# Neighbourhood attention in a two-layer diffusion backbone: keys of six heads loaded once and copied on the chip, and patterns without their unused columns

## Chip, cores, metric

The kernel runs on one core of a Trainium2 chip. The metric is the device time of one execution in microseconds. An execution is also profiled: the profile's span runs from the first to the last instruction.

## The reference

Two layers over 2048 tokens of width 1024 on a 32 x 64 grid, with 256 context tokens. The first layer joins a convolution branch and grouped-query attention; the second joins a Fourier branch and a neighbourhood attention, and the change lies in the latter alone. It has 8 heads of 64 channels. Each query at grid position (r, w) looks at 8 rows x 16 columns of keys around it, with a learned bias by relative position, and at all 256 context tokens:

```python
s_win = jnp.einsum('brqhd,brkwhd->bhrqkw', qg, kb).astype(jnp.float32) * scale \
    + bias.astype(jnp.float32)[None]
s_win = jnp.where(col_ok[:, None, :], s_win, NEG_INF).reshape(Bq, H, rows, GRID_W, kr * GRID_W)
s_ctx = jnp.einsum('brqhd,bchd->bhrqc', qg, kc).astype(jnp.float32) * scale
p = jax.nn.softmax(jnp.concatenate([s_win, s_ctx], axis=-1), axis=-1).astype(v.dtype)
...
o = jnp.einsum('bhrqkw,brkwhd->brqhd', p_win, vb) + jnp.einsum('bhrqc,bchd->brqhd', p_ctx, vc)
```

## The kernel before

The stage of interest is `natten` (L1502). Its work is cut into 32 units (h, t): head h from 0 to 7 (the title and the change count heads from 1, the code from 0), and t one of four bands of 16 grid columns. A unit has four blocks of 128 queries (8 rows x 16 columns), and a block sees 256 context keys and a window of 12 or 16 rows x 32 columns, 640 or 768 keys in all.

**Operands.** Numbers are held as a sum of two reduced-precision parts, hi and lo. The query tile `nq` [128, 2048] holds 64 channels of hi in partitions 0 to 63 and 64 channels of lo in partitions 64 to 127. Two key tiles, `nk0` (hi) and `nk1` (lo), each [128, 2304], hold the same 64 channels twice, once in each half, so that one matmul sums (hi + lo) of the query with one part of the key. All come from DRAM, where earlier stages put them (`q2_d`, `k2_d`). Each parity of h has one buffer of `nq`, `nk0` and `nk1` (pools `nk0` and `nk1`): a head's tiles take the place of those of two heads earlier, once the last score of that head has read them.

**Patterns.** The negated bias, with a huge number where a key is out of reach, lies ready in DRAM (`pat_d`). Three tiles `pat` [128, 3, 768] hold it, one per kind of band (bands 1 and 2 share one): 256 zeros for the context, then 512 window columns for each of three kinds of block. Blocks of the first and the last kind have 640 columns in all and read columns 0 to 639.

**Loads.** `load_keys(u)` (L1535) is called when the scores of the unit before u begin. For t = 0 it loads the head's queries (two DMAs of 512 KB) and keys (four of 576 KB: two parts, each into both halves); for t other than 2 it loads a pattern (768 KB). All issues of `load` have line L1539. `load_values(u)` loads the 8 x 128 values `nv` of a unit in four DMAs of 128 KB (L1571), with three buffers, and once per head those of the context (`nvc`, L1566). All stand in SP's queue. The order in SP's queue is made by a planner from program order and simulated times; only loads of the first five units keep program order.

**The stream** (L1756). TensorE, ScalarE, VectorE and GpSimd keep the order written out by hand. A unit is six steps. In step j of unit i, TensorE transposes probabilities of unit i (L1657), ScalarE and VectorE split them into hi and lo (L1662, L1664), and TensorE multiplies values with products transposed five steps earlier (L1677, L1678); scores (L1599, L1603) are made some two and a half units ahead of these, and the first score of head h comes in step 24h - 15, counted over all units from 0 as `now = 6 * i + j` (step 3 of unit 4h - 3); the last one, of its unit t = 3, in step 24h + 8. A score is evicted with its pattern by VectorE (L1611), its exponential taken by ScalarE three steps later (L1618), and scaled by GpSimd two steps after that (L1626). At a unit's end ScalarE copies the result (L1691), a DMA brings its other half to the right partitions (`ny`, L1692), and GpSimd adds the halves ten steps later (L1695). `extra(i, j)` is called at the end of each step and loads the next stage's weights near the end.

Of the kernel before, what the change touches and what calls it, by code (L numbers as in the profile page):

```python
# [11 lines left out]
F32 = mybir.dt.float32  # L12
F32R = mybir.dt.float32r
# [7 lines left out]
P = 128  # L21
D = 1024
KT = D // P
S = 2048
L = 256
T = S + L
# [3 lines left out]
HEADS = 8  # L30
# [53 lines left out]
class Build:  # L84
# [1417 lines left out]
    def natten(self):  # L1502
        nc = self.nc
        with ExitStack() as es:
# [3 lines left out]
            kp = [None, self.pool(self.n_es, "nk1", 1, side="right")]  # L1508
# [14 lines left out]
            units = [(h, t) for h in range(HEADS) for t in range(4)]  # L1523
# [3 lines left out]
            pats = []  # L1527
            for i in range(3):
                p = bp.tile([P, 3, 768], F32, name=f"pat{i}")
                nc.gpsimd.memset(p[:, :, 0:256], 0.0)  # L1530
                pats.append(p)
            heads, vals, ctxs, probs, youts, left = {}, {}, {}, {}, {}, {}

            def load_keys(u):
                h, t = u  # L1535
                first = u in units[:5]

                def load(dst, src):
                    ins = nc.sync.dma_start(dst, src)  # L1539
                    if first:  # L1540
                        self.tc.keep_in_program_order(ins)

                m, r0 = h // 2, (h % 2) * 64
                if t == 0:
                    qt = kp[h % 2].tile([P, S], F32R, name="nq", tag="nq")
                    load(qt[0:64].bitcast(F32), self.q2_d[m][0, r0 : r0 + 64])
                    load(qt[64:128].bitcast(F32), self.q2_d[m][1, r0 : r0 + 64])
                    ks = []
                    for a in range(2):
                        k = kp[h % 2].tile([P, T], F32R, name=f"nk{a}", tag=f"nk{a}")  # L1550
                        for r in range(2):
                            load(k[r * 64 : r * 64 + 64].bitcast(F32), self.k2_d[m][a, r0 : r0 + 64])
                        ks.append(k)
                    heads[h] = (qt, ks)
                if t != 2:
                    kind = kind_of[t]
                    load(
                        pats[kind][:, :, 256:768],
                        self.pat_d[:, h].rearrange("(r k) p c -> k p r c", k=3)[kind],
                    )  # L1560

            def load_values(u):
                h, t = u
# [14 lines left out]
            def scores(u):  # L1578

                h, t = u  # L1580
                if u == units[0]:
                    load_keys(u)
                if following(u):
                    load_keys(following(u))
                probs[u] = []
                for i in range(4):
                    pr = prp.tile([P, 768], F32, name="npr", tag="npr")
                    probs[u].append(pr)
                    left[id(pr)] = 1
                    yield (lambda i=i, pr=pr: score(h, t, i, pr))  # L1590
# [117 lines left out]
            def first_block():  # L1708

                bias.close()  # L1710
                qp = self.pool(self.n_es, "nq0", 1, side="right")
                y = qp.tile([P, KT, 256], F32, name="y0")
                yh, yl = (qp.tile([P, KT, 256], F32R, name=f"y0{a}") for a in "hl")
                gz = yl[:].bitcast(F32)
                self.first = y, yh, yl
                nc.sync.dma_start(gz, self.gz2_d[:, :, 0:256].rearrange("c p t -> p c t"))
                for g in range(4):
                    nc.sync.dma_start(y[:, g], self.yc_d[g][:, 0:256])
                    if g < 3:
                        nc.sync.dma_start(y[:, 4 + g], self.yd_d[g][:, 0:256])  # L1720
                for _ in range(Q1):
                    yield
                for k in range(7):
                    nc.gpsimd.tensor_tensor(out=y[:, k], in0=y[:, k], in1=gz[:, k], op=ALU.mult)
                    if k % 2 == 1 or k == 6:
                        yield
                        ks = slice(k & 6, k + 1)
                        nc.scalar.activation(yh[:, ks], y[:, ks], AF.Copy)
                        yield
                        nc.vector.tensor_tensor(  # L1730
                            out=yl[:, ks], in0=y[:, ks], in1=yh[:, ks].bitcast(F32), op=ALU.subtract
                        )

            def extra(i, j):
                if (i, j) == (28, 5):
                    even.close()
                    wo = self.pool(self.n_es, "nwo", 1, side="right")
                    self.wout = [wo.tile([P, KT, 512], F32R, name=f"wout2{a}") for a in range(2)]
                now = 6 * i + j
                k, r = divmod(now - WO0, WO1)  # L1740
                if r == 0 and 0 <= k < KT:
                    f = self.load_wout_part(self.wout_raw(wor), self.I["cd_w_out"][0], k, 0, nc.vector)
                    next(f)
                    parts.append((now + WO2, f))
                for f in [f for d, f in parts if d == now]:
                    next(f, None)
                if now == Q0:
                    parts.extend((Q0 + d, f) for f in [first_block()] for d in range(20))
                    next(parts[-1][1])

            self.stream(q, units, scores, [4] * len(units), steps, transposes, multiply, LAG, OFF, True, extra)
            for _, f in parts:
                next(f, None)
# [142 lines left out]
```

## Time and profile before

| | us |
|---|---|
| three runs | 2920.73, 2907.32, 2914.79 (median 2914.79) |
| the profiled execution | 2907.36 |
| its span | 2905.6 |
| neighbourhood attention, first score to last unit's result | 2388.7 to 2718.6 of the span |
| engines, busy share of the span | TensorE 95%, VectorE 63%, GpSimd 49%, ScalarE 38% |
| granted TensorE clock, mean | 0.977 of full speed |

A busy TensorE is not TensorE at its peak, since its matmuls are pipelined and overlap in the records. The DMA share is the mean busy share of the core's 16 DMA engines; it can pass 1, as transfers on one engine overlap. In the views PE is TensorE, PEld its weight loads, DVE VectorE, ACT ScalarE, POOL GpSimd and SP the engine whose queue issues most transfers.

### The profile page before, as it was taken

Reading aid. Unit: us, or ns where it says so; the run is one execution under the profiler, and the core shown is the slowest. Engines: PE = TensorE matmul, PEld = TensorE weight load, DVE = VectorE, ACT = ScalarE, POOL = GpSimd, SP = SyncE. Lnnn points to the kernel's source line nnn. Section 1 sums busy time; section 2 is a strip of 40 time slices with the busy share of each in tenths; the row PEclk is TensorE's granted clock in tenths of the full one; section 3 lists DMA queues with packets and bytes.
Section 4 is the critical chain, followed back from the end, with each engine's and each line's share of the span. In section 5 each row is a group of like instructions: output and inputs, shape, how many; then the busy total and the mean of one; then the engine's idle time right before and its main releaser. Section 6 shows DMA issues by size and latency. Waiting matters only on the chain.

```text
span 2905.6 us, 40946 instructions
## 1 busy us (share of the span) xinstructions
PE 2752.1 (95%) x14481; PEld 2118.0 (73%) x14481; DVE 1825.2 (63%) x2867; ACT 1116.8 (38%) x2081; POOL 1416.4 (49%) x1151
## 2 busy tenths in 40 slices
PE   7998799999999999999999999999999997889898
PEld 5988799996444444444447788988898876788787
DVE  4798868898777878878977454101212246777563
ACT  3223120312445555555553223123222236677321
POOL 2568610711666787887885652222222214445342
PEclk9999899998999999999999999999999998999999
DMA  9546332474533433321216543333434269998862
GB/s 297 192 131 207 129 123 97 135 239 151 149 107 103 144 98 106 120 68 44 73 33 210 192 159 143 138 112 112 143 132 136 82 197 230 235 230 196 270 210 80
DMA packets 346808, 432.27 MB, mean 149 GB/s; under 512 B 55900, under 2 KB 260236, under 8 KB 341611
## 3 DMA queue, kind: packets, MB, share of 16 engines
q1 hardware_dynamic: 310891, 403.03, 46.2%
q10 hardware_dynamic: 35712, 26.62, 2.9%
q8 instruction: 114, 1.87, 0.3%
q14 instruction: 91, 0.75, 0.1%
HBM read 281.87 MB, written 152.84 MB: 150 GB/s over the span
## 4 chain that ended last, share of the span: by engine, by line
PE 62%; DMA 10%; DVE 3%; POOL 2%; issue 2%; ACT 1%; SPq 0%; POOLq 0%; ACTq 0%; DVEq 0%
PE av L922 9%; PE s L907 8%; PE mm L431 6%; PE mm L433 6%; PE mm L432 6%; PE m L884 6%; PE mo L1107 4%; PE mo L1108 4%; PE mo L1109 4%; DMA nv<-v_d 3%; DMA nk<-k 3%; PE mm L442 1%; PE mm L441 1%; PE mm L440 1%; DMA pat<-pat_d 1%
## 5 line engine op out<-in xcount | busy, mean ns | idle before, releaser
L886 DVE TENSOR_REDUCE ast<-m 128x1 f32<-128x512 f32 (+1 forms) x656 | 397.9, 626 | 145.9 <-PE m L884 143.8
L912 ACT ACTIVATE pr<-s 128x512 f32<-128x512 f32 x584 | 343.2, 595 | 311.7 <-PE s L907 269.6
L947 POOL TENSOR_TENSOR accp<-accp,pr 128x512 f32<-128x512 f32 x283 | 400.1, 1414 | 86.0 <-ACT pr L912 71.3
L447 POOL TENSOR_TENSOR wlo<-wraw,whi 128x1024 fp32r<-128x1024 f32 x64 | 202.4, 3169 | 380.3 <-ACT whi L446 380.2
L533 DVE SCALAR_TENSOR_TENSOR acc<-u,cw,acc 128x1151 f32<-128x1151 f32 (+1 forms) x240 | 353.0, 1526 | 0.0
L922 PE MATMUL av<-pr,vt 128*64 128x512 f32 x1168 | 315.7, 619 | 0.0
L433 PE MATMUL mm<-hi_ab,wlo 128*128 128x384 f32 x768 | 258.7, 338 | 16.8 <-POOL wlo L447 15.5
L432 PE MATMUL mm<-lo_ab,whi 128*128 128x384 f32 x768 | 259.8, 339 | 0.0
L431 PE MATMUL mm<-hi_ab,whi 128*128 128x384 f32 x768 | 256.2, 340 | 3.3 <-ACT hi_ab L380 1.9
L431 PE MATMUL mm<-hi_cd,whi 128*128 128x512 f32 x640 | 250.8, 392 | 1.1 <-ACT hi_cd L380 1.1
L432 PE MATMUL mm<-lo_cd,whi 128*128 128x512 f32 x640 | 250.1, 391 | 0.4 <-DVE lo_cd L381 0.4
L433 PE MATMUL mm<-hi_cd,wlo 128*128 128x512 f32 x640 | 246.7, 390 | 0.0
L947 DVE TENSOR_TENSOR accd<-accd,pr 128x512 f32<-128x512 f32 x165 | 169.2, 1026 | 1.3 <-DVE accd L947 0.5
L1664 DVE TENSOR_TENSOR nlo<-npt,nhi 128x512 fp32r<-128x512 f32 x192 | 123.6, 645 | 69.3 <-ACT nhi L1662 68.5
L884 PEld LDWEIGHTS m<-k1h,q 128*128 128x128 f32 x328 | 61.8, 188 | 133.8 <-DVE ast L886 79.8
L433 PEld LDWEIGHTS mm<-hi_ab,wlo 128*128 128x128 f32 x768 | 145.5, 190 | 17.8 <-POOL wlo L447 15.8
L884 PEld LDWEIGHTS m<-k0h,q 128*128 128x128 f32 x328 | 63.5, 196 | 125.2 <-DVE ast L886 82.1
L1626 POOL TENSOR_SCALAR npr<-npr,nst 128x640 f32<-128x640 f32 (+1 forms) x128 | 108.0, 857 | 89.5 <-DVE nst L1625 64.1
L372 DVE TENSOR_SCALAR ht<-ptr,scale,shift 128x384 f32<-128x384 f32 (+2 forms) x96 | 61.2, 671 | 141.1 <-PE ptr L369 140.5
L431 PEld LDWEIGHTS mm<-hi_ab,whi 128*128 128x128 f32 x768 | 144.9, 190 | 5.3 <-ACT hi_ab L380 2.9
L432 PEld LDWEIGHTS mm<-lo_ab,whi 128*128 128x128 f32 x768 | 145.4, 189 | 0.9 <-issue 0.8
L431 PEld LDWEIGHTS mm<-hi_cd,whi 128*128 128x128 f32 x640 | 120.4, 188 | 26.1 <-ACT hi_cd L380 1.6
(321 smaller groups left out, 6931.4 us busy)
## 6 DMA issues: line engine op xcount, KB each, us to landing
wraw<-in_cd_w_in_dram SPq DMA_DIRECT2D x46, 512.0 KB, 3.8
pat_d<-big SPq DMA_DIRECT2D x72, 256.0 KB, 4.0
nk<-k SPq DMA_DIRECT2D x32, 576.0 KB, 12.7
pat<-pat_d SPq DMA_DIRECT2D x24, 768.0 KB, 6.0
nv<-v_d SPq DMA_DIRECT2D x128, 128.0 KB, 7.3
adaraw<-in_ab_w_ada_dram SPq DMA_DIRECT2D x24, 512.0 KB, 8.2
adaraw<-in_cd_w_ada_dram SPq DMA_DIRECT2D x24, 512.0 KB, 3.7
w_d<-whi SPq DMA_DIRECT2D x22, 512.0 KB, 2.8
```

The lines of the kernel that those rows point to most:

```text
L431: nc.tensor.matmul(ps, a, hh[:, k, cols], start=k == 0, stop=False)
L432: nc.tensor.matmul(ps, a, hl[:, k, cols], start=False, stop=False)
L433: nc.tensor.matmul(ps, b, hh[:, k, cols], start=False, stop=k == KT - 1)
L447: (eng or nc.vector).tensor_tensor(out=lo, in0=src, in1=hi.bitcast(F32), op=ALU.subtract)
L533: ins = nc.vector.scalar_tensor_tensor(out=acc[:, :n], in0=u[:, tap : tap + n], scalar=cw[:, ch, tap : tap + 1], in1=acc[:, :n], op0=ALU.m ...
L884: nc.tensor.matmul(ps[:, :n], lhs, kt[hp // 2][0][:, a : a + n], start=True, stop=True)
L886: nc.vector.tensor_reduce(out=s["st"][:, qt, col : col + 1], in_=ps[:, :n], axis=AX.X, op=ALU.min)
L907: nc.tensor.matmul(ps[:], kt[hp // 2][key][:, k * P : k * P + P], s[x][:].rearrange("p j n -> p (j n)"), start=key == 0, stop=key == 1,)
L912: nc.scalar.activation(pr[:], ps[:], AF.Exp, scale=-1.0)
L922: nc.tensor.matmul(s["av"][x * 64 : x * 64 + 64], vt[:, k - 1 + x, kv * 64 : kv * 64 + 64], s["pr"][k - 1 + x][:], start=k == 1, stop=k == ...
L947: eng.tensor_tensor(out=s[name][:], in0=first_in[:], in1=s["pr"][k][:], op=ALU.add)
L1664: return lambda: nc.vector.tensor_tensor(out=lo[:, :o], in0=pt[:, :o], in1=hi[:, :o].bitcast(F32), op=ALU.subtract)
```

## The change

Queries and keys get their own function, `load_head`. For heads 0 and 1 it loads as before, both halves of each key tile; head 1's loads now come when unit (0, 2) is prepared, ahead of the pattern of unit (0, 3). For heads 2 to 7 it loads the lower half of each key tile only, and it is called one head earlier in the program, when unit (h, 0) is prepared for head h + 1. The upper half is written by GpSimd: twelve copies of 64 x 384 (six for each of the two key tiles), one at the end of each of the twelve steps from 24h - 4 to 24h + 7, for head h + 1. Each pattern load becomes two DMAs: the first and the last kind of block without their last 128 columns, which no eviction reads, and the middle kind whole.

```diff
+            def load_head(h, whole):
+                m, r0 = h // 2, (h % 2) * 64
+                qt = kp[h % 2].tile([P, S], F32R, name="nq", tag="nq")
+                ks = [kp[h % 2].tile([P, T], F32R, name=f"nk{a}", tag=f"nk{a}") for a in range(2)]
+                heads[h] = (qt, ks)
+                for a in range(2):
+                    load(whole, qt[64 * a : 64 * a + 64].bitcast(F32), self.q2_d[m][a, r0 : r0 + 64])
+                for a in range(2):
+                    for r in range(2 if whole else 1):
+                        load(whole, ks[a][64 * r : 64 * r + 64].bitcast(F32), self.k2_d[m][a, r0 : r0 + 64])
+
+            PIECE = T // 6
+
+            def double(h, x):
+                a, i = divmod(x, 6)
+                k = heads[h][1][a]
+                cols = slice(i * PIECE, i * PIECE + PIECE)
+                nc.gpsimd.tensor_copy(k[64:128, cols], k[0:64, cols])
+
             def load_keys(u):
                 h, t = u
                 first = u in units[:5]
...
+                if u == units[0]:
+                    load_head(0, True)
                 if t != 2:
                     kind = kind_of[t]
-                    load(
-                        pats[kind][:, :, 256:768],
-                        self.pat_d[:, h].rearrange("(r k) p c -> k p r c", k=3)[kind],
-                    )
+                    pat = self.pat_d[:, h].rearrange("(r k) p c -> k p r c", k=3)[kind]
+                    load(first, pats[kind][:, ::2, 256:640], pat[:, ::2, 0:384])
+                    load(first, pats[kind][:, 1, 256:768], pat[:, 1])
+                if h == 0 and t == 2:
+                    load_head(1, True)
+                elif h and t == 0 and h + 1 < HEADS:
+                    load_head(h + 1, False)
...
                 now = 6 * i + j
+                h, x = divmod(now + 4, 24)
+                if 1 <= h < HEADS - 1 and x < 12:
+                    double(h + 1, x)
```

## Rows read from the trace of the kernel before

**Rows 1.** The page's chain that ended last, by line.
```profile
PE av L922 9%; PE s L907 8%; PE mm L431 6%; PE mm L433 6%; PE mm L432 6%; PE m L884 6%; PE mo L1107 4%; PE mo L1108 4%; PE mo L1109 4%; DMA nv<-v_d 3%; DMA nk<-k 3%; PE mm L442 1%; PE mm L441 1%; PE mm L440 1%; DMA pat<-pat_d 1%
```

**Rows 2.** Stretches: us; busy (count) of PE, PEld, DVE, ACT, POOL; clock, DMA, GB/s.
```profile
2425.63:2663.99 238.36, 202.28 (x1395) 188.85 (x1394) 173.56 (x435) 168.79 (x361) 109.64 (x119) 0.92 1.05 226
2466.87:2663.99 197.12, 169.09 (x1163) 157.88 (x1162) 143.72 (x361) 140.53 (x301) 92.45 (x100) 0.92 1.05 229
2430.00:2440.00 10.00, 10.00 (x78) 9.57 (x77) 9.36 (x24) 8.93 (x20) 3.52 (x5) 1.00 1.01 207
...
2490.00:2500.00 10.00, 8.65 (x47) 8.47 (x48) 3.82 (x9) 4.05 (x9) 7.42 (x8) 0.66 1.09 218
...
2580.00:2590.00 10.00, 10.00 (x78) 9.58 (x77) 9.34 (x24) 9.17 (x22) 6.52 (x8) 1.00 1.07 228
```

**Rows 3.** Waits in 2375 to 2720: us in total, times, longest.
```profile
PE nav L1677 <- DMA nv<-v_d: 33.3, 6, 7.8
...
PE ns L1599 <- DMA nk<-k: 8.3, 2, 4.2
```

**Rows 4.** Timeline of ACT: the copy that ends each unit; start, duration.
```profile
2425.63 0.60 ACT L1691 ACTIVATE ny<-nav 128x512 f32<-128x512 f32 x1 [1.14 <-PE nav L1678]
...
2466.87 0.60 ACT L1691 ACTIVATE ny<-nav 128x512 f32<-128x512 f32 x1 [0.50 <-PE nav L1678]
2474.64 0.60 ACT L1691 ACTIVATE ny<-nav 128x512 f32<-128x512 f32 x1 [0.50 <-POOL npr L1626]
2482.43 0.60 ACT L1691 ACTIVATE ny<-nav 128x512 f32<-128x512 f32 x1 [0.50 <-PE nav L1678]
2498.65 0.60 ACT L1691 ACTIVATE ny<-nav 128x512 f32<-128x512 f32 x1 [0.50 <-PE nav L1678]
...
2663.99 0.60 ACT L1691 ACTIVATE ny<-nav 128x512 f32<-128x512 f32 x1 [0.50 <-PE nav L1678]
```

**Rows 5.** DMA issues in 2360 to 2720: count, size each, median us to landing.
```profile
nk<-k SPq DMA_DIRECT2D x32, 576.0 KB, 12.7
pat<-pat_d SPq DMA_DIRECT2D x24, 768.0 KB, 6.0
nv<-v_d SPq DMA_DIRECT2D x128, 128.0 KB, 7.3
nq<-q SPq DMA_DIRECT2D x16, 512.0 KB, 11.3
```

**Rows 6.** DMA packets in 2430 to 2440, then in 2490 to 2500.
```profile
DMA packets 346, 2.07 MB, mean 207 GB/s; under 512 B 62, under 2 KB 62, under 8 KB 126
...
DMA packets 2985, 2.18 MB, mean 218 GB/s; under 512 B 194, under 2 KB 2505, under 8 KB 2984
```

**Rows 7.** Waits of SP's queue in 2375 to 2720: us in total, times, longest.
```profile
SPq L1571 <- DMA nk<-k: 46.9, 21, 2.8
...
SPq L1539 <- PE ns L1603: 5.8, 5, 2.1
```

**Rows 8.** Groups on POOL, 2380 to 2710: count | busy us, mean ns | idle before.
```profile
L1626 POOL TENSOR_SCALAR npr<-npr,nst 128x768 f32<-128x768 f32 x64 | 57.8, 907 | 62.0 <-DVE nst L1625 38.3 <-ACT nhi L1662 15.8 <-PE npt L1657 2.8
...
L1626 POOL TENSOR_SCALAR npr<-npr,nst 128x640 f32<-128x640 f32 x64 | 51.7, 808 | 27.5 <-DVE nst L1625 25.8 <-PE npt L1657 0.7 <-ACT npr L1618 0.2
...
L1695 POOL TENSOR_TENSOR yd<-ny,ny 64x512 f32<-64x512 f32 x29 | 37.2, 1282 | 85.3 <-DMA ny<-ny 52.6 <-DMA yd<-yd 15.3 <-DMA nv<-v_d 15.2
...
L1530 POOL MEMSET pat<- 128x768 f32 x3 | 2.1, 741 | 12.2 <-PE py L1480 12.2
```

**Rows 9.** Timeline of SP's queue: start, duration of the issue.
```profile
2462.24 0.47 SPq L1539 DMA_DIRECT2D nk<-k  x1
...
2467.42 1.13 SPq L1539 DMA_DIRECT2D nk<-k  x2
...
2474.12 0.48 SPq L1692 DMA_DIRECT2D ny<-ny  x1
```

**Rows 10.** Timeline of POOL: start, duration, idle time before it.
```profile
2489.87 1.26 POOL L1695 TENSOR_TENSOR yd<-ny,ny 64x512 f32<-64x512 f32 x1 [11.15 <-DMA ny<-ny]
```

More of the change, by code (lines that the diff above doesn't have):

```diff
@@ L1532, in natten, with load @@
             heads, vals, ctxs, probs, youts, left = {}, {}, {}, {}, {}, {}
+            def load(first, dst, src):
+                ins = nc.sync.dma_start(dst, src)
+                if first:
+                    self.tc.keep_in_program_order(ins)
+            def load_head(h, whole):
[14 more added lines that the diff above has]
+                nc.gpsimd.tensor_copy(k[64:128, cols], k[0:64, cols])
             def load_keys(u):
@@ L1536, in load_keys @@
                 first = u in units[:5]
[L1538 to L1554, printed above, removed]
+                if u == units[0]:
+                    load_head(0, True)
                 if t != 2:
                     kind = kind_of[t]
-                    load(
-                        pats[kind][:, :, 256:768],
-                        self.pat_d[:, h].rearrange("(r k) p c -> k p r c", k=3)[kind],
-                    )
+                    pat = self.pat_d[:, h].rearrange("(r k) p c -> k p r c", k=3)[kind]
[5 more added lines that the diff above has]
+                    load_head(h + 1, False)
             def load_values(u):
```

## The prediction

> **What bounds the kernel now.** I read the chain of waits first. TensorE holds most of it, but three loads of the neighbourhood attention stand in it by name, values (nv), keys (nk) and patterns (pat) [rows 1]; the change touches two of the three. Then the time by stretch, over this stage: while six heads pass, the 16 DMA engines are at 1.05 of their time and move 226 GB/s, and TensorE is busy in 202 of 238 us [rows 2]. A DMA share that never leaves 1 says the queue is never empty. The waits say who suffers: TensorE's multiplies for late values, 33.3 us in 6 waits, one per head, and its scores twice for keys, 8.3 us [rows 3]. The instruction that ends each unit (head, t) of the attention gives the beat [rows 4]: 7.77 us for an undisturbed unit (2466.87 to 2474.64), so 4 x 7.8 = 31.2 us for a head, but 16.2 us for the unit that waits (2482.43 to 2498.65). Six heads take 2663.99 - 2425.63 = 238.4 us, 39.7 each. So 8.5 us per head is DMA time that TensorE cannot cover, and it ends with the values because these stand in SP's queue behind the next head's burst of queries, keys and one pattern. The granted clock falls to 0.66 behind such a wait [rows 2]; while DMA sets the beat that costs nothing more.
>
> **Keys loaded once.** A key load is 576 KB, a head has four [rows 5]; two go for each of heads 3 to 8: 2 x 0.59 = 1.18 MB. Price: bytes, not instructions. In 2430 to 2440, where 220 of the 346 packets are 8 KB or longer, 207 GB/s moved; in 2490 to 2500, with 2985 mostly short packets, 218 [rows 6]; the mean is 229 [rows 2]. So 1.18 MB is 5.2 us (at 229) to 5.7 us (at 207); I take 5.4, between, since it is these very packets that ran at 207.
>
> **Narrower patterns.** A pattern of 768 KB [rows 5] becomes 640 KB: rows 0 and 2 of three lose 128 of 512 columns. Three per head: 0.39 MB, at 229 GB/s 1.7 us. The packets become shorter, not fewer, so a lower bound is 0 and an upper bound 1.9 us (at 207). Each load is now two DMAs, three more issues per head against two fewer for keys; SP issues one in about half a microsecond and mostly waits, so this I take at nothing, covered by SP's idle time; uncovered it would be 0.5 us per head.
>
> DMA per head: 39.7 - 5.4 - 1.7 = 32.6 us, still above TensorE's 31.2.
>
> **The moved load.** Queries and keys of the next head come one head earlier in the program, past four units' patterns and values on SP. But the buffer is the one of the head before the last, so no load can start until that head's last score; SP already waits there for a score, 5 times, 5.8 us in all [rows 7]. Hence no earlier start, and I take nothing. Loss if SP's order puts the load too early: it stands waiting with values queued behind it, by the same row about 1 us a time. The other queue effect is a gain inside the 5.4: values now wait 46.9 us in 21 waits at issue until a key load has landed [rows 7]. For the second head the load moves ahead of the third pattern: between 8.3 us gained (its wait goes, rows 3) and about 3 us lost (0.66 MB of pattern at 229 GB/s lands that much nearer its use); I take only the smaller first three patterns, 0.39 MB, 1.7 us gained once.
>
> **Twelve copies on POOL per head**, 64 x 384 each, from partitions 0 to 63 to 64 to 127. No row shows such a copy. From below: the fill of 2304 elements took 741 ns, 0.12 us for 384. From above: the add of 64x512 with two inputs, 1.28 us. Nearest is the one-input scaling, 907 ns for 768 and 808 for 640 elements, 0.77 ns per element [rows 8]: 808 - 256 x 0.77 = 0.61 us. 12 x 0.61 = 7.3 us per head. VectorE does 24 instructions in 9.36 and 9.34 us while POOL is busy 3.52 and 6.52 us of ten [rows 2], so I charge VectorE nothing.
>
> The Trainium skill (GPSIMD Engine Reference, Engine selection) calls one-input work on GpSimd roughly line-rate. At its 1.2 GHz that would be an estimated 0.32 us a copy; the scaling row says twice that, and the sum goes by the row. By that price POOL would have 3.5 us less to do per head, and the result would be some 1 us per head faster.
>
> The copies run in 12 consecutive steps (7.8/6 = 1.3 us each, 15.6 us), the first being due 12 steps after the buffer is free and the last two steps before the first score that needs it. In those steps POOL also has 8 scalings (6.9 us) and 2 adds (2.6 us) [rows 8]: 16.8 us of work, 1.2 late. Behind a copy that waits stand the scalings, for which the transposes wait; they run over a unit ahead, so some 8 us of lateness is hidden there. Keys do arrive: first issue 2462.24, last 2467.42 [rows 9], median 12.7 us to landing [rows 5], less once half are gone, against 15.6 us. What is late next is the add that stands ahead of the copies: it waited 11.15 us for its ny transfer, issued at 2474.12 and used at 2489.87 [rows 9, 10]. That transfer sits behind the burst, 4 x 0.59 + 2 x 0.52 + 0.79 = 4.2 MB [rows 5], which becomes 2.9 MB, 5.7 us shorter at 229 GB/s; the wait becomes 5.4 us. Copies end 1.2 + 5.4 = 6.6 us late, two steps (2.6 us) are spare, so scores come 4.0 us late if TensorE has not itself been held: 35.2 us per head. It will partly have been held by the same backlog, so the beat lies between 32.6 and 35.2; I take 33.7.
>
> **Sum.** 6 x (39.7 - 33.7) = 36.0, and 1.7 at the start: 37.7 us. The profiled execution took 2907.4 us (2905.6 of span); 2907.4 - 37.7 = 2869.7. The median of the three runs is 7.4 us higher, so as a median I give 2914.8 - 37.7 = 2877.
>
> **Rivals.**
> *TensorE's beat is reached.* Bursts and copies hide wholly, 31.2 per head, and the start loses its wait: 6 x 8.5 + 1.7 to 10 = 53 to 61 us, 2854 to 2862. For it: DMA needs just 1.4 us more per head than TensorE. Against: burst before values, add before copies.
> *Half the gain.* Waiting goes by the number of small transfers in flight, not by bytes: SP's waits for earlier landings say so; DMA share over 1 speaks against. 3.5 us per head, 21 + 1 us: 2893, between faster and the same. The case that the copies gain nothing because keys were early enough anyway belongs here: the gain can only come from bytes.
> *A fixed price per transfer.* Two fewer key loads and three more pattern issues nearly cancel. A head has 25 loads of these four kinds [rows 5] and some 5 other transfers; 30 in 39.7 us are 1.3 us each if they stood in line; one more per head is 8 us over six heads, less what the bytes still give, 10 us: 2913, the same. Against: long and short packets move alike per byte [rows 6].
> The Trainium skill (DMA: Bandwidth & Descriptors, Anatomy of one DMA) gives about 2.0 us fixed per DMA plus bytes; an estimate by it, with DMAs in line, gives two key loads as 2 x (2.0 + 1.35) = 6.7 us less, and patterns as 3 x 2.0 - 0.9 = 5.1 us more, 10 us saved over six heads. In this trace they overlap, or 30 of them would need 60 us per head where 39.7 were taken.
> *POOL becomes the bound: slower.* The add's wait stays 11.2 us and a copy costs the add's rate, 1.28 x 384/512 = 0.96 us: 12 x 0.96 + 9.5 = 21.0 us in 15.6, 5.4 late, + 11.2 - 2.6 = 14.0 per head; 45.2 against 39.7, 6 x 5.5 less 1.7: 31 us slower, 2946. It decides from a lateness of 39.7 - 31.2 = 8.5 us per head. For: the wait lies exactly ahead of the copies. Against: it is itself a product of the backlog.
>
> **How the numbers follow.** A measurement of this kernel can tell about 0.5%, 14.6 us, from no change. Chances: forecast 0.58, TensorE's beat 0.13, half 0.14, fixed price 0.06, POOL 0.09. Faster: 0.58 + 0.13 + half of 0.14 = 0.78; the same: 0.07 + 0.06 = 0.13; slower 0.09. The range takes in the forecast's beats of 32.6 to 35.2, the TensorE case and the half case's upper part: 2852 to 2907.
>
> **What would show it.** Unit ends: a head's beat of 33 to 35 us. The wait of multiplies for values falls from 33 us to under 12; window rates stay near 220 GB/s with a share near 1, on 17% fewer bytes (1.57 of 39.7 us x 226 GB/s = 9.0 MB per head). Copies: 72 of about 0.6 us. Scores waiting for the copies over 4 us per head, or copies over 0.9 us, would make the forecast wrong on the slow side; a DMA share well under 1 with a beat of 31.2 on the fast side.

## The result, and the profile after

| | before | after |
|---|---|---|
| median of four runs, us | 2916.62 | 2870.23 |
| lowest to highest | 2907.32 to 2920.73 | 2867.47 to 2876.44 |
| the profiled execution | 2907.36 | 2871.33 |
| its span | 2905.6 | 2869.4 |

The ratio of the runs is 0.9857, 95% interval 0.983 to 0.9884: the kernel is faster by 1.4%. The two medians stand 46 us apart, the two profiled executions 36 us. The attention stage alone is 38.0 us shorter: first score to the end of unit (0, 0) took 36.9 us before and 34.9 after, the six heads up to the end of unit (6, 0) 238.4 and 203.7, the seven units behind it 54.6 and 53.3. What stands before and behind the stage is 1.8 us longer. All of these are differences between the starts of the copies that end the units.

The stretches of the kernel after, the six heads first (columns as in [rows 2]: busy time and count of PE, PEld, DVE, ACT and POOL, clock, DMA share, GB/s):

```profile
2424.94:2628.62 203.68, 194.99 (x1395) 181.34 (x1394) 172.42 (x433) 169.12 (x361) 144.10 (x189) 0.97 1.02 218
...
2480.00:2490.00 10.00, 9.36 (x69) 8.40 (x68) 8.69 (x22) 8.17 (x18) 9.12 (x14) 1.00 0.98 224
...
2500.00:2510.00 10.00, 10.00 (x74) 9.36 (x73) 8.90 (x23) 9.19 (x23) 1.70 (x2) 1.00 1.11 274
2510.00:2520.00 10.00, 6.09 (x43) 5.19 (x42) 5.91 (x16) 5.21 (x12) 7.19 (x11) 0.90 1.14 237
2540.00:2550.00 10.00, 10.00 (x78) 9.58 (x78) 9.36 (x24) 9.15 (x21) 8.12 (x12) 1.00 1.11 224
```

In these 203.68 us 44.5 MB moved (218 GB/s); before it was 53.9 MB in 238.36 us (226 GB/s, [rows 2]). So 17.5% of the bytes went and 14.6% of the time, and the DMA engines are still at 1.02. TensorE has the same matmuls in 195 us of 204. GpSimd's busy time rose from 109.6 to 144.1 us. The third and fourth line are a place to remember: in 2500 to 2510 GpSimd does two instructions in ten microseconds, and just behind it TensorE falls to 6.09.

TensorE's waits in the six heads, for [rows 3] (us in total, times, longest):

```profile
PE npt L1670 <- POOL npr L1639: 7.1, 6, 1.7
PE ns L1616 <- POOL nk L1558: 1.1, 2, 0.6
PE nav L1690 <- issue: 0.4, 1, 0.4
```

The 33.3 us of matmuls waiting for values are gone, all six waits. In their place come short waits for GpSimd: transposes wait for scaled probabilities, scores for copied keys. In the start of the stage one wait replaced another:

```profile
PE nav L1690 <- DMA nvc<-v_d: 8.9, 1, 8.9
```

Before it was two waits for the second head's keys, 8.3 us [rows 3]; those keys now go ahead of the first values, and the first values are late.

The units' ends, for [rows 4]:

```profile
2424.94 0.60 ACT L1704 ACTIVATE ny<-nav 128x512 f32<-128x512 f32 x1 [0.45 <-PE nav L1691]
...
2490.83 0.60 ACT L1704 ACTIVATE ny<-nav 128x512 f32<-128x512 f32 x1 [0.51 <-PE nav L1691]
...
2514.34 0.60 ACT L1704 ACTIVATE ny<-nav 128x512 f32<-128x512 f32 x1 [0.50 <-POOL npr L1639]
2529.40 0.60 ACT L1704 ACTIVATE ny<-nav 128x512 f32<-128x512 f32 x1 [0.50 <-DMA nk<-k]
...
2560.60 0.60 ACT L1704 ACTIVATE ny<-nav 128x512 f32<-128x512 f32 x1 [0.50 <-PE nav L1691]
...
2628.62 0.60 ACT L1704 ACTIVATE ny<-nav 128x512 f32<-128x512 f32 x1 [0.50 <-PE nav L1691]
```

The mean is 33.9 us per head, but the heads differ: from (0, 0) on, periods of 33.5, 32.4, 38.6, 31.2, 36.8 and 31.2 us. Two heads reach TensorE's own 31.2, two are at 37 to 39. The third period holds one unit of 15.1 us (2514.34 to 2529.40).

What GpSimd does there: the add that stands ahead of the copies, one per head (start, duration, idle before):

```profile
2442.91 1.29 POOL L1708 TENSOR_TENSOR yd<-ny,ny 64x512 f32<-64x512 f32 x1 [6.07 <-DMA ny<-ny]
...
2475.08 1.30 POOL L1708 TENSOR_TENSOR yd<-ny,ny 64x512 f32<-64x512 f32 x1 [4.66 <-DMA ny<-ny]
...
2512.27 1.29 POOL L1708 TENSOR_TENSOR yd<-ny,ny 64x512 f32<-64x512 f32 x1 [9.43 <-PE ns L1616]
...
2541.47 1.29 POOL L1708 TENSOR_TENSOR yd<-ny,ny 64x512 f32<-64x512 f32 x1 [0.21 <-PE npt L1670]
...
2580.12 1.29 POOL L1708 TENSOR_TENSOR yd<-ny,ny 64x512 f32<-64x512 f32 x1 [7.67 <-DMA ny<-ny]
...
2610.73 1.30 POOL L1708 TENSOR_TENSOR yd<-ny,ny 64x512 f32<-64x512 f32 x1 [1.45 <-DMA ny<-ny]
```

The length of a head follows this wait: 6.07, 4.66, 9.43, 0.21, 7.67 and 1.45 us of waiting stand beside heads of 33.5, 32.4, 38.6, 31.2, 36.8 and 31.2 us. In the first two heads the profile names the transfer of the other half (`ny`). The third and the fifth are the first add of a new pair of heads. The result tile `yd` has one buffer; this add must also wait until the store of the pair before it (1 MB, issued at 2504.60 and 2572.34) has read it. The names behind the arrow are those of whatever ended last by the profile; the kernel before has the same add waiting 15.35 us for `yd<-yd` in one of these places. Behind the add stand GpSimd's copies and scalings, for which TensorE waits in the rows above.

GpSimd's groups, for [rows 8]:

```profile
L1639 POOL TENSOR_SCALAR npr<-npr,nst 128x768 f32<-128x768 f32 x64 | 58.3, 911 | 39.6 <-DVE nst L1638 28.6 <-ACT nhi L1675 4.9 <-ACT wout L446 2.6
...
L1708 POOL TENSOR_TENSOR yd<-ny,ny 64x512 f32<-64x512 f32 x30 | 39.1, 1302 | 30.9 <-DMA ny<-ny 19.9 <-PE ns L1616 9.4 <-PE npt L1670 0.2
L1558 POOL CAST nk<-nk 64x384 fp32r<-64x384 f32 x72 | 34.9, 502 | 3.1
```

The 72 copies take 502 ns each and wait for nothing worth the name (3.1 us in all): the keys are there when a copy is due.

Transfers, for [rows 5] (count, size each, median us to landing):

```profile
nk<-k SPq DMA_DIRECT2D x20, 576.0 KB, 8.2
pat<-pat_d SPq DMA_DIRECT2D x24, 384.0 KB, 6.0
nq<-q SPq DMA_DIRECT2D x16, 512.0 KB, 7.6
pat<-pat_d SPq DMA_DIRECT2D x24, 256.0 KB, 5.1
```

Twelve key loads fewer, and a key load lands in 8.2 us where it took 12.7.

### The profile page after: what moved, and what is told of

Read it like the earlier page. It is cut to its first block, busy times and chain, and to the rows that moved or that the text cites. A ratio compares the mean times of both kernels' runs of the same rounds, so it can differ in the third digit from the quotient of the medians.

```text
span 2869.4 us, 41078 instructions
## 1 busy us (share of the span) xinstructions
PE 2741.3 (96%) x14481; PEld 2107.3 (73%) x14481; DVE 1823.9 (64%) x2867; ACT 1117.7 (39%) x2081; POOL 1451.9 (51%) x1223
## 4 chain that ended last, share of the span: by engine, by line
PE 67%; DMA 4%; DVE 3%; POOL 2%; issue 2%; ACT 1%; SPq 0%; POOLq 0%; ACTq 0%; DVEq 0%
PE av L922 9%; PE s L907 8%; PE mm L433 6%; PE m L884 6%; PE mm L431 6%; PE mm L432 6%; PE mo L1107 4%; PE mo L1108 4%; PE mo L1109 4%; PE npt L1670 3%; PE ns L1616 2%; PE nav L1691 1%; PE nav L1690 1%; PE mm L440 1%; PE mm L442 1%
```

## The experiments

Each was run on one chip beside the kernel before. A kernel's time over all of its stages varies more than the effects looked for, so beside the median stand the stage's own times, from the unit ends of its profile: the start (first score to the end of (0, 0)), six heads (to the end of (6, 0)), and these divided by six.

| kernel | median, us | ratio to before, interval | start | six heads | per head |
|---|---|---|---|---|---|
| before | 2916.6 (beside the others 2910.4 to 2911.5) | | 36.9 | 238.4 | 39.7 |
| after | 2870.2 | 0.9857 (0.983 to 0.9884) | 34.9 | 203.7 | 33.9 |
| keys only | 2884.9 | 0.9903 (0.9881 to 0.9925) | 34.0 | 211.6 | 35.3 |
| patterns only | 2904.6 | 0.9985 (0.9967 to 1.0003) | 34.9 | 232.6 | 38.8 |
| move only | 2908.3 | 0.9987 (0.997 to 1.0005) | 34.0 | 237.1 | 39.5 |
| split only | 2915.8, one run | | 35.5 | 243.8 | 40.6 |
| few patterns, before | 2864.5, one run | | 36.7 | 190.0 | 31.7 |
| few patterns, after | 2863.9, one run | | 36.1 | 187.2 | 31.2 |
| copies twice | 2891.1, one run | | 36.4 | 223.8 | 37.3 |
| half stores, after | 2876.4 | 0.9881 (0.9861 to 0.9902) | 34.3 | 198.8 | 33.1 |
| half stores, before | 2926.5, one run | | 35.1 | 238.8 | 39.8 |
| second head once | 2876.3 | 0.9873 (0.9855 to 0.9891) | 29.1 | 206.3 | 34.4 |
| both of these | 2875.0 | 0.9865 (0.9843 to 0.9887) | 29.6 | 201.6 | 33.6 |
| half stores, other half by ScalarE | 2885.9 | 0.9912 (0.9893 to 0.993) | 33.9 | 210.9 | 35.2 |

### The change in parts

**Keys only.**

```diff
-                    load(first, pats[kind][:, ::2, 256:640], pat[:, ::2, 0:384])
-                    load(first, pats[kind][:, 1, 256:768], pat[:, 1])
+                    load(first, pats[kind][:, :, 256:768], pat)
```

> Keys of heads 3 to 8 loaded once and copied as in the change, patterns loaded whole in one transfer each as before. Theory A (bytes on the DMA engines set the beat of a head, 39.7 us before and 33.9 us after): 1.18 of the 1.57 MB saved per head stay saved, so 24 to 32 us less than before, a beat of 34.5 to 35.7 us. Theory B (the number of transfers sets it): two of 30 transfers fewer per head, 2 x 1.3 us x 6 = 16 us less. Theory C (the earlier place of the loads in the program sets it): the whole gain of some 36 us.

**Patterns only.** In the kernel before:

```diff
-                    load(
-                        pats[kind][:, :, 256:768],
-                        self.pat_d[:, h].rearrange("(r k) p c -> k p r c", k=3)[kind],
-                    )
+                    pat = self.pat_d[:, h].rearrange("(r k) p c -> k p r c", k=3)[kind]
+                    load(pats[kind][:, ::2, 256:640], pat[:, ::2, 0:384])
+                    load(pats[kind][:, 1, 256:768], pat[:, 1])
```

> Patterns without the unused columns in two transfers each as in the change, all keys loaded twice as before. Theory A (bytes): 0.39 MB less per head, 8 to 11 us less in all, a beat of about 38 us. Theory B (number of transfers): three more per head, 3 x 1.3 x 6 = 23 us more. Theory C (place): no change within 5 us.

**Move only.** Against the kernel after, with the pattern loaded in one transfer as in keys only:

```diff
-                    for r in range(2 if whole else 1):
+                    for r in range(2):
...
-                if 1 <= h < HEADS - 1 and x < 12:
-                    double(h + 1, x)
```

> Loads of queries and keys called at the place that the change gives them, but both halves of every key by DMA, no copies, patterns whole in one transfer. Theory A (bytes): a beat of 39 to 40 us, within 6 us of before in all, since the buffer is not free sooner. Theory C (place): some 36 us less, as after the change. Theory B: as A, since the number is that of before.

**Split only.** In the kernel before, the same two loads with all columns:

```diff
+                    load(pats[kind][:, ::2, 256:768], pat[:, ::2])
+                    load(pats[kind][:, 1, 256:768], pat[:, 1])
```

> The kernel before with each pattern loaded whole but in two transfers. Theory A (bytes): a beat within 0.5 us of 39.7, within 3 us in all. Theory B (a price per transfer of 1.3 us): three more per head, a beat of 43.6 us, some 23 us more; with 2 us each 36 us more.

The six heads in the stretches of keys only:

```profile
2429.33:2640.89 211.56, 196.99 (x1395) 182.14 (x1394) 173.94 (x435) 169.59 (x361) 143.98 (x190) 0.97 1.01 226
```

and of patterns only:

```profile
2427.16:2659.78 232.62, 202.07 (x1395) 189.13 (x1395) 172.24 (x433) 168.80 (x360) 109.81 (x119) 0.93 1.06 221
```

Keys alone give 26.8 us over the six heads, patterns alone 5.7, the sum 32.5 of the 34.7 that both give. The rate is near that of before in all of them (226 and 221 GB/s against 226): 47.8 and 51.4 MB instead of 53.9, and per megabyte 4.42 us before, 4.43 with keys only, 4.52 with patterns only, 4.58 after. The move alone gives 1.2 us over six heads, so the earlier place in the program (theory C) is out: the buffer decides when the load starts. The fourth head's first key load is issued 3.1 us after the end of unit (0, 3) with the move, 3.2 us before it. The gain of patterns only in runs, 0.9985 with an interval that reaches 1, is no difference by itself.

Splitting a pattern into two whole transfers cost 5.4 us over six heads, 18 extra transfers, 0.3 us each. That is not the 1.3 us of theory B, whose 23 us are out. That it is more than nothing is likely, but not shown: it is one profile, heads of that kernel range from 37.3 to 43.4 us, and its one whole run, 2915.8, lies among those of before. It fits patterns only: at the mean rate the narrower patterns should give 1.7 us per head, 10.3 in all; 5.7 came, and the difference is about what the split would cost. A megabyte took 4.51 us with the split (54.1 MB), about as with patterns only; half stores below, with the same split in the kernel after, are at 4.45.

### Are they bytes, whichever they are

**Few patterns.** In the kernel before, and in the kernel after, the pattern is loaded for the first head alone; the other heads use it too, so that their own bias is left out.

```diff
-                if t != 2:
+                if t != 2 and h == 0:
```

> The kernel before without the pattern loads of heads 2 to 8 (left out: their own bias; they use the first head's), so 2.36 of 9.0 MB per head less and nothing added to GpSimd. Theory A (bytes, whichever they are): DMA needs 29 us per head, so the beat falls to TensorE's 31.2 to 33, 40 to 50 us less in all, and the multiplies' wait for values goes. If it is the key loads themselves that hold up the values: 3 x 1.3 us per head or less, under 25 us in all.

> The change without the pattern loads of heads 2 to 8 (left out: their own bias; they use the first head's). DMA then needs some 25 us per head, far under TensorE's 31.2, so what a head takes over the 31.7 us of the same kernel without copies is the price of the copies when DMA is not in the way. Theory A with hidden copies: 31.2 to 32.2 us per head. If GpSimd with its copies is a bound of its own: 33 us or more per head, with scores or transposes waiting for GpSimd.

The six heads of the first, in the kernel before:

```profile
2433.09:2623.05 189.96, 188.31 (x1395) 177.12 (x1394) 171.26 (x432) 168.19 (x360) 110.32 (x119) 1.00 0.99 202
```

and of the second, in the kernel after:

```profile
2432.81:2620.04 187.23, 187.23 (x1395) 177.07 (x1394) 171.75 (x433) 167.99 (x361) 143.91 (x190) 1.00 0.78 168
```

Without touching a key, the kernel before falls to 31.7 us per head: its keys are still loaded twice, and the matmuls' wait for values is gone. So it is the bytes in the queue, not the key loads; and 18 transfers fewer at 1.3 us would have given 23 us, not 48. One thing more is in that line: the DMA share is still 0.99, though TensorE is busy in 188.3 of 190.0 us and waits for no load. The rate has fallen to 202 GB/s. A share at 1 does not by itself say that DMA sets the beat; the waits for loads do. The second is the floor in its pure form: with 0.78 of DMA TensorE is busy in all of 187.23 us, with no wait of its own in the list of waits, and GpSimd makes its 72 copies at 77% of its time. The copies alone cost nothing.

### How much room the copies have

**Copies twice.** In the kernel after:

```diff
                 if 1 <= h < HEADS - 1 and x < 12:
                     double(h + 1, x)
+                    double(h + 1, x)
```

> The change with each of the twelve copies made twice: 6 us more on GpSimd per head in 12 steps of 1.3 us. If the copies are hidden by a wide margin: within 3 us of the change. By the sum of the prediction (15.6 us hold 6.9 of scalings, 2.6 of adds and now 12 of copies, 5.9 too many, 2.6 spare before the scores): 3 us per head, 15 to 25 us more, with scores waiting for the copies.

TensorE's waits in the six heads of this kernel:

```profile
PE ns L1616 <- POOL nk L1558: 13.9, 12, 1.9
PE npt L1670 <- POOL npr L1639: 7.5, 6, 1.7
```

20.1 us more over six heads than the change, 3.4 per head, for 6 us more of copies: the sum of work in those twelve steps, which gave 3, holds. Scores wait for copied keys twice per head. The three heads whose add ahead of the copies waits 4.9 to 5.5 us take 38.5 to 39.8 us, the three whose add waits for nothing 35.1 to 36.1. GpSimd is thus the next bound: there is room for twelve copies of half a microsecond beside its other work, and none for twelve more.

### What is left

**Half stores.** The result tile is allocated once and stored half by half, in the kernel after and in the kernel before:

```diff
-                    youts[m] = yp.tile([P, S], F32, name="yd", tag="yd")
+                    youts[m] = youts[m - 1] if m else yp.tile([P, S], F32, name="yd", tag="yd")
...
-                    if h % 2 == 1 and t == 3:
-                        nc.sync.dma_start(self.yd_d[m][:], y[:])
+                    if t == 3:
+                        nc.sync.dma_start(self.yd_d[m][a], y[a])
```

> The change, and the result tile of two heads is stored half by half, each half at the end of its head, from one tile that stays, so that the first add of the next pair of heads no longer waits for the store of the whole tile. Theory D (after the change, bytes set the beat no more; what is left of the waits is GpSimd standing at this add in the third and fifth head, 38.6 and 36.8 us where the fourth and sixth take TensorE's 31.2): both fall to 31.2 to 33, 8 to 13 us less than the change, some 45 to 50 us less than before. Theory A alone (bytes still set it): as many bytes, within 3 us of the change.

> The kernel before with the result stored half by half in the same way. Theory A (bytes set the beat before): no less than 39 us per head, within 4 us of before in the stage, though GpSimd's wait of 15 us for the store goes. Theory D' (GpSimd's waits set it before too): 8 us or more less.

The six heads of half stores in the kernel after,

```profile
2429.19:2628.03 198.84, 191.10 (x1395) 176.86 (x1394) 172.49 (x433) 169.32 (x361) 142.04 (x187) 1.00 1.07 225
```

and the add ahead of the copies in each of them:

```profile
2447.37 1.29 POOL L1708 TENSOR_TENSOR yd<-ny,ny 64x512 f32<-64x512 f32 x1 [6.30 <-DMA ny<-ny]
...
2479.09 1.30 POOL L1708 TENSOR_TENSOR yd<-ny,ny 64x512 f32<-64x512 f32 x1 [4.20 <-DMA ny<-ny]
...
2513.61 1.28 POOL L1708 TENSOR_TENSOR yd<-ny,ny 64x512 f32<-64x512 f32 x1 [6.71 <-DVE nst L1638]
...
2547.12 1.30 POOL L1708 TENSOR_TENSOR yd<-ny,ny 64x512 f32<-64x512 f32 x1 [6.04 <-PE nav L1691]
...
2578.80 1.30 POOL L1708 TENSOR_TENSOR yd<-ny,ny 64x512 f32<-64x512 f32 x1 [3.93 <-DVE nlo L1677]
...
2612.28 1.30 POOL L1708 TENSOR_TENSOR yd<-ny,ny 64x512 f32<-64x512 f32 x1 [5.95 <-PE nav L1691]
```

The two slow heads fall from 38.6 and 36.8 to 34.2 and 31.5 us as theory D has it, so the store did hold up their add. But the fourth and sixth rise from 31.2 to 33.8 and 33.7, so that of the 9.7 us that went from the two only 4.8 stay: 33.1 us per head with DMA at 1.07. The lines show why. With half stores the add waits in every head, 3.9 to 6.7 us, and the length of a head goes with that wait: 6.30, 4.20, 6.71, 6.04, 3.93 and 5.95 us beside 33.7, 32.0, 34.2, 33.8, 31.5 and 33.7. The store of the whole tile is gone, two of the six lines name the other half's transfer, and it was issued 12 to 15 us before each of these adds. So in all likelihood it is this transfer, among the loads of the burst in SP's queue, that holds the add. Shorter waits are hidden: 2.55 us in the kernel with half stores and the second head's keys once, 2.70 and 3.07 in the kernel after with few patterns, left the head at 31.2 us.

So both theories hold half: the store shaped the beat in two heads, and the bytes act in the others, through the transfer that stands among them. That bytes by themselves would set 32.6 us per head, as the prediction worked it out, is not shown. The seven units behind the six heads take 56.1 us instead of 53.3, and over a whole run the gain doesn't show: 2876.4 against 2870.2 in other rounds, ratios 0.9881 and 0.9857 with intervals that overlap. In the kernel before half stores give nothing, 238.8 against 238.4: there the late loads decide. Its one run, 2926.5, is long for what stands ahead of the stage: the first score comes at 2404.8 us instead of 2388.7.

**The other half by ScalarE**, on top of half stores:

```diff
-                nc.sync.dma_start(y3[a], y2[o])
+                nc.scalar.dma_start(y3[a], y2[o])
```

> The result stored half by half, and the transfer of a unit's other half issued by ScalarE's queue right behind the copy that makes it, so that it stands behind nothing in SP's queue. If GpSimd's waits for that transfer still set part of the beat of 33.1 us: 31.5 to 32.5 us per head, 4 to 10 us less than with half stores alone. Theory A (bytes set 32.6 us per head): within 3 us of 33.1 x 6. If ScalarE, busy 9 of 10 us, feels the issues: up to 0.3 us per unit more.

This lost 12.1 us over six heads, 8.6 of them in the first (42.3 us). GpSimd's adds no longer wait, but ScalarE does, against an expected 0.3 us per unit. Its exponentials in the six heads, which in the kernel after have no idle time before them (busy us, mean ns, idle before):

```profile
L1631 ACT ACTIVATE npr<-npr,nst 128x640 f32<-128x640 f32 (+1 forms) x96 | 85.2, 887 | 38.9 <-DVE nst L1624 12.4 <-DMA nv<-v_d 7.8 <-DMA yd<-yd 6.1
```

and pieces of its timeline:

```profile
2441.48 0.47 ACTq L1705 DMA_DIRECT2D ny<-ny  x1
2442.00 0.83 ACT L1631 ACTIVATE npr<-npr,nst 128x640 f32<-128x640 f32 x1 [7.77 <-DMA nv<-v_d]
...
2566.95 0.60 ACT L1704 ACTIVATE ny<-nav 128x512 f32<-128x512 f32 x1 [0.41 <-issue]
2569.66 0.47 ACTq L1705 DMA_DIRECT2D ny<-ny  x1
2570.17 0.83 ACT L1631 ACTIVATE npr<-npr,nst 128x640 f32<-128x640 f32 x1 [2.62 <-DMA nk<-k]
```

By the profile's releasers the issue itself waits until another transfer has landed (here values, then a key load), and ScalarE, with 9 of 10 us of work in an undisturbed stretch [rows 2], stands behind it: 7.8 us in the first head, 2.6 us in the other place. The transposes then wait for what ScalarE and VectorE make, 11.7 us in the six heads. The expectation did not have a wait at the issue.

**The second head's keys once**, in the kernel after, and together with half stores:

```diff
-                    load_head(1, True)
+                    load_head(1, False)
...
+                if 0 <= now < 6:
+                    double(1, 2 * now)
+                    double(1, 2 * now + 1)
```

> The change with the second head's keys too loaded once and copied, two copies in each of the first six steps: 1.18 MB less before the first values. Theory A (bytes, at the start of the stage too): TensorE's wait of 8.9 us for the first head's context values falls by some 5 us, 4 to 6 us less than the change. If the twelve copies early on hold up GpSimd's first scalings: no gain, or up to 5 us lost.

> Half stores and the second head's keys loaded once, together: if both gains stand, 0 to 10 us less than the change, 45 to 55 us less than before.

In the start TensorE's wait for the first values is now:

```profile
PE nav L1690 <- DMA nvc<-v_d: 1.5, 1, 1.5
```

7.4 us less, and the start takes 29.1 us instead of 34.9, about as the bytes have it: 1.18 MB at 226 GB/s are 5.2 us. But the six heads take 206.3 us instead of 203.7. The combination takes 29.6 + 201.6 us to the end of (6, 0) where the change takes 34.9 + 203.7, 7.4 us less in one profile; the seven units behind take 55.4 us instead of 53.3. Its first head takes 40.2 us, with 9.8 us of waiting at the add ahead of the copies. Over whole runs it isn't to be told from the change: 2875.0 against 2870.2, ratios 0.9865 and 0.9857. No version here is shown to beat the change.

Why whole runs hide 7 us: what stands ahead of this stage, which none of these kernels touches, differs between the profiled executions. The multiplies of the first layer's attention in the kernel after (durations ns, first and last start):

```profile
L922 PE MATMUL av<-pr,vt x1168: 592/618/1116, 708.3 to 1535.9; 128*64 128x512 f32 x195
```

and with the second head's keys once:

```profile
L922 PE MATMUL av<-pr,vt x1168: 592/643/1116, 713.5 to 1544.3; 128*64 128x512 f32 x195
```

8.4 us later at the end, long before the stage has begun, and 5.2 of them already at the start of these multiplies. Whether that goes with the program or with the execution is not shown: runs of before alone reach from 2897 to 2921 us.

## Why the prediction was right

**The size and the signs.** The multiplies' wait for values was to fall under 12 us and is gone in the six heads; 72 copies, 1.1 us of scores waiting for them, 218 GB/s on 17.5% fewer bytes. 37.7 us were forecast against the profiled execution, 36.0 were measured; as a median 2877, measured 2870.2, inside the range. The medians moved by 46 us because the profiled execution of before lay 9.3 us under its median and that of after 1.1 us above; the profiles' difference is the one that the sum was made for.

**What bounds the kernel.** That late loads set the beat holds: without most patterns it falls to 31.7 us in the kernel before and to TensorE's 31.2 in the kernel after, while neither the moved load nor half stores change the kernel before (39.5 and 39.8). The reason given, a DMA share that never leaves 1, was too strong: few patterns has 0.99 in the kernel before with TensorE as the bound. The waits for values and keys carried the argument.

**Keys, 5.4 us per head.** Keys only gives 26.8 / 6 = 4.5, with the copies and the late add in it. The price by bytes holds: 4.42 us per megabyte before, about the same after it, 4.6 in the forecast. But 6.1 MB went in that stretch, not 6 x 1.18 = 7.1; why is not shown (loads issued ahead of the stretch that land in it are one way). That the twelve copies by themselves hide is shown by few patterns: 31.2 us per head with them.

**Patterns, 1.7 us per head, and the split at nothing.** Mis-sized: 1.0 per head was measured for both together. The split was taken as covered, with 0.5 uncovered; one profile gives 0.9 per head, 0.3 per transfer. If that holds, the narrower columns are worth 1.9, about what was said.

**The moved load, nothing.** 0.2 us per head: right, and for the reason given.

**Copies, 0.61 us.** They took 0.502. The one-input scaling was the right neighbour; 0.61 is a fifth too dear. The bound from below was misread: each fill [rows 8] writes 768 elements (three times 256 context columns), not 2304, so that 741 ns give 0.37 us for 384, not 0.12. An estimate by the Trainium skill's line rate (GPSIMD Engine Reference, Engine selection) was 0.32; the trace lies between that and 0.61. VectorE was not slowed: 24 instructions in 9.36 us before [rows 2], and 24 in 9.36 us again in 2540 to 2550 of the kernel after, beside 8.12 us of GpSimd with its copies.

**What is late next: the add ahead of the copies.** Right engine, right instruction, and the right transfer in part. The wait was put at 5.4 us in every head, for the other half's transfer behind the burst. In the kernel after it is 4.9 in the mean, but unevenly: 6.1 and 4.7 for that transfer in the first two heads, 9.4 and 7.7 in the third and fifth, where the store of the result tile comes in, and little in the fourth and sixth. With half stores the add waits in every head, 5.5 us in the mean and in all likelihood for that transfer, as the prediction had it, and a head takes 33.1. How much of the wait is hidden was put too low: 1.4 us, where waits of up to 3 us cost nothing (cheaper copies give 1.3 of the difference). So 33.7 against 33.9 is partly luck: the store, which the sum did not have, adds 0.8, and the number was taken from the middle of 32.6 to 35.2.

**The start, 1.7 us.** 2.0 measured, but this tells little: move only, with whole patterns, has 2.9 less, and half stores in the kernel before, whose start is not changed, 1.8 less. The wait for keys went, as one end of the bounds had it, and a wait for values of about the same length came.

**The rivals.** TensorE's beat was reached in two heads of six and, with fewer bytes, in all. A fixed price per transfer of 1.3 us does not stand in this queue: a split cost about 0.3 in one profile. Nor does one of 2.0 us, as the Trainium skill has it (DMA: Bandwidth & Descriptors, Anatomy of one DMA; fitted there on transfers issued from GpSimd, where these are issued from SP). Half the gain did not happen: the wait went with the bytes. GpSimd did not make the kernel slower, but it is where TensorE now waits, and copies twice shows how little room is left: 0.96 us a copy, as that rival had it, are 5.5 us more per head than 0.5, nearly the 6 us that cost 3.4 us per head there.

## What to carry to other kernels

Where the compute engine waits for late loads and the DMA share stays at 1 through a stage, price an edit by its bytes at the stage's own rate, and look for the wait that goes at the loads which stand last in the queue, not at the loads that were cut. The share alone is not enough: it was 0.99 in a kernel that TensorE bound. A copy on an engine with idle time can buy such bytes, but count the work of that engine in the very steps where the copies stand, with what stands ahead of them in order. When the mean of a stage moves as forecast, still look at its single periods, and set each beside the wait that you think sets it: here a small transfer behind the big ones held two heads, a store two others, and the last two ran free.

## What the runs showed that was not expected

A GpSimd copy of 64 x 384 from partitions 0 to 63 to partitions 64 to 127 takes 499 to 512 ns. A transfer issued from ScalarE's queue made ScalarE stand 2.6 us, once 7.8, since by the profile the issue waits for an earlier transfer's landing; in SP's queue such waits (46.9 us in 21, [rows 7]) hold up only what is issued behind them. With the DMA share at 1.05, cutting a transfer of 768 KB in two cost about 0.3 us, in one profile. A wait of GpSimd of up to 3 us per head cost TensorE nothing, and one of 6 to 10 us cost 2 to 9 us. And a stage that no edit touches, the first layer's attention, ended anywhere from 1534 to 1549 us in the profiles of these kernels, more than most of the effects looked for.
